# Time steps' sums and one group's y transposes one large product later; weights-stationary products in runs of sixteen matmuls of equal width

## The chip, the cores and the metric

The kernel runs on one core of one Trainium2 chip. The metric is the device time of one execution in microseconds (us); lower is better. Times are given as the median of several runs with the lowest and the highest. One further execution was taken by the hardware profiler; the profile's rows come from that one.

Five engines work in parallel, each through its own queue in order: TensorE (PE; its weight loads are shown apart as PEld), VectorE (DVE), ScalarE (ACT), GpSimd (POOL) and SyncE (SP, which here only starts DMAs). TensorE writes to PSUM, which has eight banks of 128 x 512 float32; VectorE and ScalarE read from there.

## The reference

It is a decoder trunk of two layers on 256 positions of width 1024. Each layer is a SwiGLU FFN (half step), a token mixer, a second FFN and a gated per-layer embedding. All weights and results are float32.

```python
for i in range(DEPTH):                                   # 2
    h = h + 0.5 * swiglu(rmsnorm(h, ffn1_norm[i]), ffn1_wg[i], ffn1_wu[i], ffn1_wd[i])
    h = h + hybrid_mixer(rmsnorm(h, mix_norm[i]), w_in[i], ...)
    h = h + 0.5 * swiglu(rmsnorm(h, ffn2_norm[i]), ffn2_wg[i], ffn2_wu[i], ffn2_wd[i])
    gate = jax.nn.sigmoid(rmsnorm(h, ple_norm[i]) @ ple_w_gate[i])
    h = h + gate * (p[i] @ ple_w_proj[i])
return rmsnorm(h, final_norm)

def hybrid_mixer(u, w_in, ...):
    proj = u @ w_in
    sc_b, sc_c, sc_x, m_z, m_xbc, m_dt, gate_a, gate_m = jnp.split(proj, PROJ_SPLITS, axis=-1)
    y_a = (sc_b * causal_depthwise_conv(sc_c * sc_x, sc_conv_w)) @ sc_w_out
    xbc = jax.nn.silu(causal_depthwise_conv(m_xbc, m_conv_w) + m_conv_b)
    xs, bm, cm = jnp.split(xbc, (SSM_INNER, SSM_INNER + SSM_GROUPS * SSM_STATE), axis=-1)
    dt = jax.nn.softplus((m_dt + m_dt_bias).astype(jnp.float32))
    y = ssd_chunked(xh * dt[..., None], A * dt, bm, cm)  # 32 heads, 4 groups, chunks of 128
    y = (y + m_D[:, None] * xh).reshape(b, s, SSM_INNER)
    y_m = grouped_rmsnorm(y * jax.nn.silu(m_z), m_norm, SSM_GROUPS) @ m_w_out
    merged = jax.nn.sigmoid(gate_a) * y_a + jax.nn.sigmoid(gate_m) * y_m
    return merged @ w_o
```

In `ssd_chunked` the running sums of `A * dt` within a chunk of 128 positions (`a_cum`) give the decays: within the chunk, to its end, and from one chunk to the next.

## The kernel before

**Products.** Each float32 operand is split into a high part (rounded to the fast float32 form, `hi`) and the rest (`lo`), and a product is made of three: hi x hi, hi x lo, lo x hi. The weights come in chunks of two halves, each 128 x 1024. SyncE fetches a half (`fetch`, L113), ScalarE makes `whi` and VectorE `wlo` of it (`half`, `split`, L94 to L127). Up to seven halves are live (`NHALF`), so the load runs over two chunks ahead of the product that reads them; a half's place is reused when its last reader on TensorE is done.

There are two forms. In the activations-stationary form (`as_`, L248) the activations are loaded into the array and 512 columns of weights stream past; all its matmuls have 512 columns. It makes the FFNs' down products, the head of each stage, z, the gates and the output products. In the weights-stationary form (`wide_ws`, L236) 128 columns of weights are loaded, and the activations of all 256 positions stream past. For `whi` the moving operand is `both[:, k]`, high and low part of the activations side by side, 512 columns; for `wlo` it is the high part alone, 256 columns. `xx` is the activations' tile. One such product takes one chunk: for each of two blocks of 128 output columns (b = 0, 1; one PSUM bank each) eight matmuls of 512 and eight of 256 columns over k = 0 to 7. The list `FOURS` (L234) orders each block's sixteen: 2 wide, 4 narrow, 4 wide, 4 narrow, 2 wide; block 0 is done before block 1 begins. Left and right half of a bank are then added up (ScalarE copies one half, VectorE adds the other: `both_parts`, L391, in the FFN; `Mixer.wide`, L843).

The FFN's up products use this form for chunks 4 to 21 (`up`, L406), and in the mixer it makes bc (4 products), xs (8) and sc (12).

`drip` (L208) puts small matmuls of the mixer's heads (`xd` times `m`, 64 columns, one per head) between those of the large products: `wide_ws` lets up to four go in the middle and up to four at the end of each block, `as_` two at its end.

**Order of the mixer.** `ORDER` (L40) is a list by hand of the forty large products of a mixer. After the n-th of them the small steps follow that `side` (L756) has for n. `EARLY = (1, 4)`: after product 1 `steps` (VectorE and ScalarE make `dt` and `av`), after product 4, sc0.1, `sums` (L936). `sums` has three fp32 products on TensorE with `av` (each shown as two matmuls), copies of them by VectorE (`acT`, `acum`, `w0`), two exponentials on ScalarE, and a DMA on ScalarE's queue that writes `acT` to DRAM as `acD`. `decay` later reads `acD` back, broadcast to all partitions, as `m`, by a DMA on ScalarE's queue too. Products 5 and 6 are bc10 and sc0.2.

For each group g of heads `LAGS[g]` (L43) says how many large products after the second xs product of g a step comes. For group 2 that product is xs5, number 21; `y_turn0` and `y_turn1` have lag 8, and so come after number 29, xs7. `y_turn` (L1036) transposes the finished y of one chunk on TensorE into one bank (`flip`, L271), ScalarE copies the bank to `yh`, and VectorE makes `yl` from bank and `yh`. Its input y comes from `gain` (L1032) on VectorE. Number 30 is z3.0 (activations-stationary; its two banks are held up to z3.1, number 33), and `turn0`, `overlap` and `decay0` of group 3 follow it; number 31 is gm0.0. ga1.0, number 28, holds two banks up to number 34.

The eight banks are one pool (`bank`, L76); a step that needs one waits until a former user's last reader is done. The framework that builds the program sets the order of instructions within each engine's queue by their dependences and their place in the program, so that on ScalarE and VectorE instructions of neighbouring steps are interleaved.

Of the kernel before, what the change touches and what calls it, by code (L numbers as in the profile page):

```python
# [16 lines left out]
P = 128  # L17
# [5 lines left out]
KD = D // P  # L23
# [15 lines left out]
LEAD = 8  # L39
ORDER = ("bc8 sc0.0 xs0 sc0.1 bc10 sc0.2 xs1 sc1.0 sc1.1 sc1.2 xs2 xs3 z1.0 sc2.0 sc2.1 z1.1 sc2.2 xs4 bc9 bc11 xs5 "  # L40
         "z2.0 z2.1 sc3.0 xs6 sc3.1 sc3.2 ga1.0 xs7 z3.0 gm0.0 so0.0 z3.1 ga1.1 gm0.1 so1.0 gm1.0 gm1.1 so0.1 so1.1").split()
EARLY = (1, 4)
LAGS = [  # L43
# [16 lines left out]
def trunk(ctx: ExitStack, tc: tile.TileContext, a: dict, out: bass.AP):  # L60
# [15 lines left out]
    def bank():  # L76
        return psp.tile([P, 512], F32, tag="ps", name=nm("ps"))

    def mm(o, l, r, start, stop):
        return nc.tensor.matmul(o, lhsT=l, rhs=r, start=start, stop=stop).ins  # L80
# [55 lines left out]
    def chunk(name, i, c, kn):  # L136

        key = (name, i, c)
        sources[key] = (a[name][i, c], kn)
        return key  # L140
# [67 lines left out]
    def drip(n=1):  # L208
        for _ in range(min(n, len(fill))):
            fill.pop(0)()  # L210
# [20 lines left out]

    FOURS = [(k, s) for s, ks in enumerate((range(2), range(4), range(2, 6), range(4, 8), range(6, 8))) for k in ks for s in (s % 2,)]  # L234

    def wide_ws(o, wc, cols, x):  # L236
        xh, _, both = x
        for n, (k, s) in enumerate(FOURS):
            if n == KD + 2:
                drip(KD // 2)  # L240
            if s == 0:
                mm(o, wc[k][0][:, cols], both[:, k], k == 0, k == KD - 1)
            else:
                mm(o[:, 0:256], wc[k][1][:, cols], xh[:, k], False, False)
        drip(KD // 2)


# [136 lines left out]
    class FFN:  # L384
        def __init__(self, i, gu, dn, gname, ple=None):
# [3 lines left out]
            hh, hl, banks, acc, head_pr = {}, {}, {}, {}, {}  # L389
# [7 lines left out]
            def evac(j):  # L397
                gate, pr = both_parts(banks[j][0], "sg"), both_parts(banks[j][1], "pr")
                del banks[j]
                nc.scalar.activation(gate, gate, AF.Silu)  # L400
                nc.vector.tensor_tensor(pr, gate, pr, op=ALU.mult)
                hh[j] = fp.tile([P, 256], F32R, tag=f"hh{j}", name=nm("hh"))
                hl[j] = fp.tile([P, 256], F32R, tag=f"hl{j}", name=nm("hl"))
                split(hh[j], hl[j], pr)

            def up(j):  # L406
                def f(wc):
                    banks[j] = [bank(), bank()]
                    for b in range(2):
                        wide_ws(banks[j][b], wc, slice(b * P, (b + 1) * P), prep.x)  # L410
                    evac(j)
                return f, [chunk(gu, i, j, KD)]

# [44 lines left out]
            n = NF // 2  # L458
# [141 lines left out]
    class Mixer:  # L600
        def __init__(self, i):
# [150 lines left out]
            for c in range(NT):  # L752
                small[f"turn{c}"] = lambda g, c=c: xs_turn(2 * g + c)
                for what in ("decay", "scale", "outputs", "skip", "chain", "gain", "y_turn"):
                    small[what + str(c)] = lambda g, c=c, f=getattr(S, what): f(g, c)
            side = {EARLY[0]: [S.steps], EARLY[1]: [S.sums]}  # L756
            for g in range(NG):
# [10 lines left out]
            def wide(name, x, done, kd=KD, upto=None, extra=()):  # L768
# [23 lines left out]
                if upto:  # L792
                    return acc, [([], [run(c, [0]) for c in range(nch - STAG, nch)]),
                                 ([run(c, [1]) for c in range(nch - STAG, nch - 1)], [run(nch - 1, [1])])]

            S.ym, S.mo_tail = wide("w_mo", of_y, None, kd=2 * KD, upto=True)
            S.wo = Narrow("w_o", i, lambda: S.mt)
            self.tail = S.wo.tail
# [44 lines left out]
        def wide(self, wc, what):  # L843

            pss = [bank(), bank()]
            for b in range(2):
                wide_ws(pss[b], wc, slice(b * P, (b + 1) * P), self.prep.x)
            v = self.t2(what)
            for b in range(2):
                o = v[:, b * 256:(b + 1) * 256]  # L850
                nc.scalar.activation(o, pss[b][:, 256:512], AF.Copy)
                nc.vector.tensor_tensor(o, o, pss[b][:, 0:256], op=ALU.add)
            return v
# [230 lines left out]
    for s in stages[1:] + [None]:  # L1084
        prep = s.prep if s else Last(a["final_norm"])
# [80 lines left out]
```

## Time and profile before

| | |
|---|---|
| median of 3 runs | 1535.74 us (1530.8 to 1536.1) |
| the profiled execution, time | 1531.25 us |
| the profiled execution, span | 1529.5 us |
| PE, DVE, ACT busy | 99%, 68%, 62% of the span |
| mean granted TensorE clock | 0.997 |
| DMA | 285.59 MB, 187 GB/s |

How to read it: the span goes from the first instruction to the last. A busy TensorE means that some matmul is under way; matmuls overlap, each being issued while the one before still drains, so their lengths (0.39 us for 512 columns) are longer than the distance of their starts, and the distance of the starts is the pace. In a row of the timeline stand the start, the length of the merged group, the engine, the line, the operation, the output and inputs by the program's names, the shapes and the count. Brackets show how long the engine sat idle before, and what ended that. The granted clock is 1.00 when TensorE runs at full speed.

### The profile page before, as it was taken

The numbers are of one execution on the slowest core, as the hardware profiler recorded it, in microseconds if no ns is written. First come the engines' busy times: TensorE is split into PE (matmuls) and PEld (weight loads), VectorE is DVE, ScalarE is ACT, GpSimd is POOL, SyncE is SP. The second block draws the span as 40 slices with busy tenths as digits, with TensorE's granted clock in tenths as the row PEclk, the third lists the DMA queues.
The fourth block names the chain that finished last, engine by engine and source line by source line (L and its number), as shares of the span: only waits on it lengthen the run. The fifth ranks groups of instructions, "written<-read, shape, count | busy, mean of one in ns | idle before, by whom it ended". The sixth has DMA issues, their size and how long they took to land.

```text
span 1529.5 us, 20958 instructions
## 1 busy us (share of the span) xinstructions
PE 1507.4 (99%) x7793; PEld 1272.1 (83%) x7793; DVE 1043.7 (68%) x1511; ACT 944.7 (62%) x1472; POOL 24.6 (2%) x41
## 2 busy tenths in 40 slices
PE   9999999999999999999999999999999999999998
PEld 6888887888888888888878888888888888888886
DVE  6666467989865576664676655688888555767545
ACT  6665367879854356653666654687888543666544
POOL 0000000000000000000000000000000000000000
PEclk9999999999999999999999999999999999999999
DMA  7656564556556556656565565655555565665642
GB/s 268 213 190 189 172 206 156 192 184 198 188 160 187 195 191 197 192 193 193 164 211 180 190 193 163 208 190 176 194 193 181 164 193 176 217 191 185 190 158 90
DMA packets 85432, 285.59 MB, mean 187 GB/s; under 512 B 10577, under 2 KB 10961, under 8 KB 85330
## 3 DMA queue, kind: packets, MB, share of 16 engines
q1 hardware_dynamic: 77968, 267.94, 54.5%
q10 hardware_dynamic: 7362, 16.31, 3.2%
q8 instruction: 61, 1.00, 0.3%
q14 instruction: 41, 0.34, 0.1%
HBM read 283.10 MB, written 1.11 MB: 186 GB/s over the span
## 4 chain that ended last, share of the span: by engine, by line
PE 90%; DVE 5%; ACT 2%; issue 2%; DMA 0%; POOL 0%; POOLq 0%; ACTq 0%; DVEq 0%
PE ps L80 88%; DVE wlo L96 3%; PE ps L277 1%; ACT whi L98 1%; DVE xn L333 1%; PE ps L638 0%; DMA m<-acD 0%; POOL rstd L293 0%; ACT junk L325 0%; DVE ac L863 0%; DVE xx L281 0%; ACT m L981 0%; PE ps L439 0%; DVE h L538 0%; DVE y L1034 0%
## 5 line engine op out<-in xcount | busy, mean ns | idle before, releaser
L96 DVE TENSOR_TENSOR wlo<-raw,whi 128x1024 fp32r<-128x1024 f32 x508 | 615.8, 1221 | 335.3 <-ACT whi L98 324.1
L98 ACT ACTIVATE whi<-raw 128x1024 fp32r<-128x1024 f32 x508 | 534.0, 1058 | 275.0 <-PE ps L80 241.5
L80 PE MATMUL ps<-xx,whi 128*128 128x512 f32 x1920 | 538.2, 398 | 0.0
L80 PE MATMUL ps<-whi,xx 128*128 128x512 f32 (+1 forms) x1168 | 369.7, 392 | 2.4 <-ACT whi L98 1.5
L80 PEld LDWEIGHTS ps<-xx,whi 128*128 128x128 f32 x1920 | 327.0, 189 | 45.5 <-issue 3.8
L80 PEld LDWEIGHTS ps<-xx,wlo 128*128 128x128 f32 x1920 | 294.5, 189 | 40.3
L80 PE MATMUL ps<-xx,wlo 128*128 128x256 f32 x1920 | 306.3, 281 | 0.0
L80 PEld LDWEIGHTS ps<-whi,xx 128*128 128x128 f32 x1168 | 217.9, 188 | 48.4 <-ACT whi L98 2.8
L80 PE MATMUL ps<-wlo,xx 128*128 128x512 f32 (+1 forms) x584 | 222.6, 388 | 0.3 <-DVE wlo L96 0.3
L80 PE MATMUL ps<-whi,hh 128*128 128x512 f32 x352 | 137.3, 390 | 0.0
L80 PE MATMUL ps<-wlo,hh 128*128 128x512 f32 x352 | 137.0, 389 | 0.0
L80 PEld LDWEIGHTS ps<-wlo,xx 128*128 128x128 f32 x584 | 109.9, 188 | 22.8 <-DVE wlo L96 1.8
L80 PE MATMUL ps<-whi,hl 128*128 128x512 f32 x352 | 113.7, 389 | 0.0
L80 PEld LDWEIGHTS ps<-whi,hl 128*128 128x128 f32 x352 | 66.1, 188 | 13.8
L80 PEld LDWEIGHTS ps<-wlo,hh 128*128 128x128 f32 x352 | 66.1, 188 | 13.7
L80 PEld LDWEIGHTS ps<-whi,hh 128*128 128x128 f32 x352 | 66.1, 188 | 13.6
L393 ACT ACTIVATE sg<-ps 128x256 f32<-128x256 f32 x72 | 27.7, 385 | 54.7 <-PE ps L80 54.7
L400 ACT ACTIVATE sg<-sg 128x256 f32<-128x256 f32 x72 | 30.0, 416 | 33.1 <-DVE sg L394 33.1
L80 PE MATMUL ps<-whi,yh 128*128 128x512 f32 x128 | 50.0, 390 | 0.0
L80 PE MATMUL ps<-wlo,yh 128*128 128x512 f32 x128 | 49.8, 389 | 0.0
L293 POOL TENSOR_TENSOR rstd<-var,mhalf 128x1 f32<-128x1 f32 x34 | 23.6, 696 | 1500.0 <-DVE var L287 998.5
L325 ACT ACTIVATE junk<-h 128x512 bf16<-128x512 f32 (+1 forms) x37 | 22.6, 612 | 39.3 <-DVE h L538 28.4
(162 smaller groups left out, 1209.1 us busy)
## 6 DMA issues: line engine op xcount, KB each, us to landing
raw<-in_gu SPq DMA_DIRECT2D x176, 512.0 KB, 4.2
raw<-in_dn SPq DMA_DIRECT2D x88, 512.0 KB, 3.9
raw<-in_w_xbc SPq DMA_DIRECT2D x48, 512.0 KB, 4.1
raw<-in_w_sc SPq DMA_DIRECT2D x48, 512.0 KB, 4.0
raw<-in_w_z SPq DMA_DIRECT2D x32, 512.0 KB, 3.7
raw<-in_w_mo SPq DMA_DIRECT2D x32, 512.0 KB, 3.7
raw<-in_w_ga SPq DMA_DIRECT2D x16, 512.0 KB, 4.3
m<-acD ACTq DMA_DIRECT2D x16, 512.0 KB, 4.6
```

The lines of the kernel that those rows point to most:

```text
L80: return nc.tensor.matmul(o, lhsT=l, rhs=r, start=start, stop=stop).ins
L96: return nc.vector.tensor_tensor(lo, src, hi.bitcast(F32), op=ALU.subtract).ins
L98: up = nc.scalar.activation(hi, src, AF.Copy).ins
L277: nc.tensor.transpose(tp[:, j * P:(j + 1) * P], src[:, c:c + P], ident)
L293: nc.gpsimd.tensor_tensor(r, v, mhalf, op=ALU.pow)
L325: self.squared = nc.scalar.activation(junk[:, 0:sl.stop - sl.start], h[t][:, sl], AF.Square, scale=1.0 / 32.0, accum_out=ss).ins
L333: ins = nc.vector.scalar_tensor_tensor(xn[:, sl], h[t][:, sl], r, g, op0=ALU.mult, op1=ALU.mult)
L393: nc.scalar.activation(v, ps[:, 256:512], AF.Copy)
L400: nc.scalar.activation(gate, gate, AF.Silu)
```

## The change

```diff
-EARLY = (1, 4)
+EARLY = (1, 5)
 LAGS = [
...
-     ("skip1", 4), ("y_turn0", 8), ("y_turn1", 8), ("chain1", 5), ("gain1", 6), ("gain0", 7),],
+     ("skip1", 4), ("y_turn0", 9), ("y_turn1", 9), ("chain1", 5), ("gain1", 6), ("gain0", 7),],
...
-    FOURS = [(k, s) for s, ks in enumerate((range(2), range(4), range(2, 6), range(4, 8), range(6, 8))) for k in ks for s in (s % 2,)]
-
-    def wide_ws(o, wc, cols, x):
+    LONG_RUNS = [(b, k, s) for s, ks in ((0, range(KD - 1)), (1, range(KD)), (0, range(KD - 1, KD))) for b in range(2) for k in ks]
+
+    def wide_ws(os, wc, x):
         xh, _, both = x
-        for n, (k, s) in enumerate(FOURS):
-            if n == KD + 2:
+        for n, (b, k, s) in enumerate(LONG_RUNS):
+            cols = slice(b * P, (b + 1) * P)
+            if n in (KD - 1, 2 * KD - 2, 3 * KD - 2):
                 drip(KD // 2)
             if s == 0:
-                mm(o, wc[k][0][:, cols], both[:, k], k == 0, k == KD - 1)
+                mm(os[b], wc[k][0][:, cols], both[:, k], k == 0, k == KD - 1)
             else:
-                mm(o[:, 0:256], wc[k][1][:, cols], xh[:, k], False, False)
+                mm(os[b][:, 0:256], wc[k][1][:, cols], xh[:, k], False, False)
         drip(KD // 2)
...
                     banks[j] = [bank(), bank()]
-                    for b in range(2):
-                        wide_ws(banks[j][b], wc, slice(b * P, (b + 1) * P), prep.x)
+                    wide_ws(banks[j], wc, prep.x)
                     evac(j)
...
             pss = [bank(), bank()]
-            for b in range(2):
-                wide_ws(pss[b], wc, slice(b * P, (b + 1) * P), self.prep.x)
+            wide_ws(pss, wc, self.prep.x)
```

The sums come after product 5, bc10, instead of 4, sc0.1. Group 2's two y transposes come after number 30, z3.0, instead of 29, xs7.

`wide_ws` now takes both banks and orders all 32 matmuls of a product: seven wide of block 0, seven wide of block 1, eight narrow of block 0, eight narrow of block 1, then the last wide one of each block. The next product begins with fourteen wide ones, so that where two such products follow each other without anything between, sixteen wide matmuls stand in a row, and sixteen narrow ones within each product. Both banks are complete only at the product's end. The head products may go in after matmul 7, 14, 22 and 32, four at a time, where before it was after 10 and 16 of each block.

## The prediction

> **What bounds the kernel now.** I read the page first, then the view of waits for TensorE, then its timeline. The page says that TensorE is nearly never without work:
>
> ```profile
> span 1529.5 us, 20958 instructions
> ...
> PE 1507.4 (99%) x7793; PEld 1272.1 (83%) x7793; DVE 1043.7 (68%) x1511; ACT 944.7 (62%) x1472; POOL 24.6 (2%) x41
> ...
> PE 90%; DVE 5%; ACT 2%; issue 2%; DMA 0%; POOL 0%; POOLq 0%; ACTq 0%; DVEq 0%
> ```
>
> So time can go in two ways only: TensorE's matmuls follow each other more closely, or its few waits vanish. The view of waits lists the latter (total us, times, longest):
>
> ```profile
> PE ps L80 <- DVE av L933: 5.5, 2, 2.8
> PE ps L277 <- DVE xn L333: 2.4, 5, 1.4
> PE ps L277 <- DVE y L1034: 2.0, 2, 1.0
> ...
> PE ps L80 <- ACT whi L98: 1.5, 3, 0.7
> ...
> PE ps L80 <- DVE wlo L96: 0.3, 1, 0.3
> ```
>
> The first row is the wait of the sums (they multiply `av`), once per layer; the third is that of group 2's y transposes, once per layer. The change moves exactly these two. The last row says that the split weights come in time almost always.
>
> For the pace I read TensorE's timeline in the first FFN (start, length, xcount), where the alternating runs of four stand alone:
>
> ```profile
> 121.09 1.09 PE L80 MATMUL ps<-xx,whi 128*128 128x512 f32 x4
> 122.02 0.64 PE L80 MATMUL ps<-xx,wlo 128*128 128x256 f32 x4
> 122.50 1.09 PE L80 MATMUL ps<-xx,whi 128*128 128x512 f32 x4
> ...
> 126.70 1.09 PE L80 MATMUL ps<-xx,whi 128*128 128x512 f32 x4
> ```
>
> I take starts, since lengths overlap. Four 512-column matmuls take 122.02 - 121.09 = 0.93 us, 0.2325 each; four of 256 columns 0.48, 0.120 each. From 121.09 to 126.70 lies one product (16 of each): 5.61 us. Where the up products end and the all-512 down products begin, the pace changes:
>
> ```profile
> 136.53 0.63 PE L80 MATMUL ps<-xx,whi 128*128 128x512 f32 x2
> 137.00 0.39 PE L80 MATMUL ps<-whi,hh 128*128 128x512 f32 x1
> ...
> 137.92 0.62 PE L80 MATMUL ps<-whi,hl 128*128 128x512 f32 x2
> ...
> 139.28 0.62 PE L80 MATMUL ps<-whi,hl 128*128 128x512 f32 x2
> ```
>
> 137.92 to 139.28 is one period of six: 1.36 us, 0.2267 each. The six from 136.53 to 137.92, right behind a run of 256, took 1.39. So a 512 run needs about six matmuls to settle, and loses about 0.03 us on the way. That this is no property of the weights-stationary form shows where such a product follows a long 512 run:
>
> ```profile
> 35.10 0.61 PE L80 MATMUL ps<-xx,whi 128*128 128x512 f32 x2
> 35.55 0.64 PE L80 MATMUL ps<-xx,wlo 128*128 128x256 f32 x4
> ```
>
> Its first two take 0.45 us, 0.225 each; only behind the first 256 run do they slow to 0.2325.
>
> **The runs of sixteen.** The change adds and drops no matmul. How many there are, by the page:
>
> ```profile
> L80 PE MATMUL ps<-xx,whi 128*128 128x512 f32 x1920 | 538.2, 398 | 0.0
> ...
> L80 PE MATMUL ps<-xx,wlo 128*128 128x256 f32 x1920 | 306.3, 281 | 0.0
> ```
>
> 1920 / 16 = 120 products: 18 in each of four FFNs, 24 in each of two mixers. Each goes from eight width changes to two. Afterwards 16 wide matmuls cost 16 x 0.2267 + 0.03 = 3.657 us. For a long run of 256 the trace has only the dt product, with half as many stationary columns:
>
> ```profile
> 221.53 2.03 PE L80 MATMUL ps<-xx,dtw 128*64 128x256 f32 x16
> 223.40 0.63 PE L80 MATMUL ps<-xx,whi 128*128 128x512 f32 x2
> ```
>
> 1.87 / 16 = 0.117 each. The narrow matmul with 128 columns is bounded by 0.117 and 0.120; I take 0.119, nearer the row with the same stationary shape: 1.904 us. The product becomes 5.561, a gain of 0.049. Some ten products are cut by interposed head products (the drips keep their count, four of four a product) and gain little, so I count 110: **-5.4 us**. Ends: with 0.117, 5.527 us and -9.5; if the wide run never settles (0.2325 x 16 + 1.904 = 5.624), +1.5.
>
> The Trainium skill, "TensorE: Matmul & The Clock Gate", section "Wait — 56ns, not 53.3ns?", speaks against this part: start to start is N / 2.4 GHz plus a fixed 2.5 ns or so, whatever stands beside it. By it (an estimate from that page) a product is 16 x 215.8 + 16 x 109.2 ns = 5.20 us in any order, and this term would be 0. The rows above disagree, in the size and in that the same width takes 0.225 or 0.2325 by its neighbours.
>
> What the new order does to others: both banks of a product now end with it, so the first bank's copy and add, which ran beside the second half, come 2.8 us later, in line with the second's. In an FFN they fit:
>
> ```profile
> 126.70:132.31 5.61, 5.61 (x34) 4.90 (x33) 3.96 (x7) 3.90 (x7) 0.00 (x0) 1.00 0.59 193
> ```
>
> VectorE is busy 3.96 and ScalarE 3.90 of the 5.61 us, and the output is needed only in the down stage, the bank four products on. I cost it at 0; cover gone, it is one copy more on the way, 385 ns:
>
> ```profile
> L393 ACT ACTIVATE sg<-ps 128x256 f32<-128x256 f32 x72 | 27.7, 385 | 54.7 <-PE ps L80 54.7
> ```
>
>  The low halves of the weights are first read at matmul 14 instead of 2, which only helps; the second high half is read at 4 instead of 8, about 0.5 us sooner, and the loads run over two products ahead.
>
> **The sums, one product on.** Windows of the two stalls (span, PE, PEld, DVE, ACT, POOL, granted clock, DMA):
>
> ```profile
> 246.00:250.00 4.00, 1.25 (x8) 0.60 (x6) 3.74 (x9) 3.58 (x6) 0.00 (x0) 1.00 0.33 110
> 250.00:257.60 7.60, 7.60 (x35) 6.59 (x36) 4.53 (x11) 2.81 (x6) 0.00 (x0) 0.78 0.70 225
> 1003.27:1007.30 4.03, 1.28 (x8) 0.68 (x6) 3.66 (x9) 3.50 (x6) 0.00 (x0) 1.00 0.37 117
> 1007.30:1014.00 6.70, 6.70 (x41) 5.92 (x41) 4.66 (x12) 3.40 (x8) 0.00 (x0) 1.00 0.73 213
> ```
>
> 4.00 - 1.25 and 4.03 - 1.28: 2.75 us idle each. Behind the first stall the granted clock is 0.78 over 7.6 us, 1.7 us lost; behind the second it is 1.00. One product on is 5.6 us, over twice the lateness, so both go: 5.5 + 1.7 = **-7.2 us**. The Trainium skill, same page, section "HAM oscillation — how this bites in real kernels", has the rule of no idle gaps over about 3.4 us. Read strictly it gives no loss to a gap of 2.75 and 1.7 us less to win (a sum of 1521); the first window disagrees, the third agrees.
>
> What is late next? The six fp32 matmuls of the sums, VectorE's copies, ScalarE's exponentials and one DMA write of `acD` move along. On ScalarE's queue the read of `m` waits for that write, and everything of ScalarE waits behind it:
>
> ```profile
> 254.65 1.28 ACT L950 ACT_TABLE_LOAD   x1 [2.45 <-DMA acD<-acT]
> ```
>
> Now the 2.45 us lie where ScalarE had little to do (2.81 of 7.60); afterwards they fall in the next product, before this one:
>
> ```profile
> 263.00:269.00 6.00, 6.00 (x35) 5.22 (x34) 5.71 (x9) 5.91 (x11) 0.00 (x0) 1.00 0.62 178
> ```
>
> ScalarE is full there. The weights are far enough ahead, but group 0's states product is not:
>
> ```profile
> 285.45 0.58 ACT L639 ACTIVATE xg<-ps 128x512 f32<-128x512 f32 x1
> ...
> 286.06 0.69 DVE L987 TENSOR_TENSOR xw<-xg,w 128x512 f32<-128x512 f32 x1 [0.17 <-ACT xg L639]
> ...
> 286.86 1.07 PE L80 MATMUL ps<-xw,btok 128*128 128x512 f32 x2
> ```
>
> `xw` ends at 286.75, and TensorE uses it at 286.86: no slack. A late ScalarE makes a new wait of 0 to 2.45 us a layer; I take 1.0, nearer the lower end, since ScalarE does the rest of its work with gaps: **+2.0 us**.
>
> **Group 2's y transposes.** In the first mixer:
>
> ```profile
> 414.06 0.74 DVE L1034 SCALAR_TENSOR_TENSOR y<-y,rstd,mn 128x512 f32<-128x512 f32 x1
> ...
> 414.95 1.06 PE L277 MATMUL ps<-ident,y 128*128 128x128 f32 x8 [1.01 <-DVE y L1034]
> ...
> 417.60 1.06 ACT L280 ACTIVATE yh<-ps 128x512 fp32r<-128x512 f32 x2
> ...
> 420.45 1.28 DVE L281 TENSOR_TENSOR yl<-ps,yh 128x512 fp32r<-128x512 f32 x2
> ...
> 422.25 0.48 PE L80 MATMUL ps<-whi,xx 128*128 128x512 f32 x1
> ```
>
> The wait of 1.01 goes, twice: -2.0. But the two banks are free only when `yl` is done, at 421.73, and the product gm0.0 starts at 422.25. Moved to after z3.0, the transposes stand 2.5 us or less before gm0.0, while ga1 and z3 hold two banks each and `turn0`, `overlap` and the two transposes the other four: all eight. gm0.0 must wait for one of these copies. Bounds 0 (copies at once: about 0.5 + 0.6 + 0.7 us) and 4 us (as late as here: 422.25 - 414.95 = 7.3, less 2.5, and some); I take 0.5 a layer, since VectorE has no `yl` of its own before it then: **-1.0 us** net.
>
> Sum: -5.4 - 7.2 + 2.0 - 1.0 = -11.6 on the profiled execution's 1531.25 us (span 1529.5): 1519.6, say **1520**. That execution is 4.5 us under the median of the three (1535.74; 1530.8 to 1536.1). A clock drop after the second layer's stall too would be 1.7 of it, and would go with the stall; the rest I can't place, so it is kept for the upper end.
>
> **Rivals.**
> 1. Both widths settle (narrow at 0.117): -9.5 instead of -5.4, 1515. For: the dt row; against: its loads are half as wide.
> 2. Spacing goes by a matmul's own width and form alone (0.2325 and 0.119 in these products, whatever the order): the runs give nothing, 1519.6 + 5.4 = 1525. For: products in both stages have one period; against: the rows at 35.10 and 137.92. (The rule of the Trainium skill on the gap, "TensorE: Matmul & The Clock Gate", is of this kind.)
> 3. The stalls move instead of going: states late by the full 2.45 us in both layers, gm0.0 by 2 us: 2 x 1.45 + 2 x 1.5 = 5.9 more, 1525.5. For: the full ScalarE, the full banks.
> 4. Slower: VectorE becomes the bound of the mixers. Its queue is in order; an add that waits for the product's end can hold up what stands behind it.
>
> ```profile
> 223.00:330.00 107.00, 103.99 (x591) 88.67 (x590) 89.09 (x163) 83.02 (x148) 1.72 (x2) 0.98 0.55 176
> ```
>
> It has 17.9 us to spare in 107, 19 products of 5.6 us: 0.94 us each. If the later first add costs it over 0.94 us in each of the 48 mixer products, the rest is paid; from 0.94 + 11.6 / 48 = 1.18 us on the kernel is slower, at 1.5 it is 1519.6 + 48 x 0.56 = 1546. Against: TensorE waited 0.3 us in all for `wlo`, and the weights run two products ahead.
>
> **How the numbers follow.** Chances: forecast 0.43, rival 1 0.17, rival 2 0.20, rival 3 0.13, rival 4 0.07. The range 1511 to 1529 takes in the first four with some microseconds around them (below: rival 1 with no new waits, 1512; above: rival 3 with most of the 4.5) and leaves out rival 4. Half a per cent, 7.7 us, is about what a measurement can tell: faster means under 1528. That is nearly all of the forecast and rival 1 (0.57 of 0.60), most of rival 2 (0.13) and half of rival 3 (0.07): 0.77. What is left of these is within: 0.03 + 0.07 + 0.06 = 0.16. Slower is rival 4, 0.07.
>
> **What would show it.** Right: product period 5.56 instead of 5.61; no row `av` and no `y` L1034 in the waits; clock 1.00 behind the sums. Wrong: a period of 5.61 or more (rival 2), 5.53 (rival 1), new rows of waits for `xw` L987, `yh` or `yl` (rival 3), or many waits for `wlo` in the mixers (rival 4).

## The result, and the profile after

The changed kernel takes 1522.28 us (median of 6 runs, 1521.07 to 1528.09); the kernel before, measured beside it, 1533.12 us (6 runs, 1530.8 to 1536.1). The ratio is 0.9935, with an interval of 0.9914 to 0.9957: about 10 us faster. The profiled execution took 1522.78 us, its span is 9.1 us shorter than before.

The page of the changed kernel, with the same rows as shown of before:

```profile
span 1520.4 us, 21065 instructions
...
PE 1501.2 (99%) x7793; PEld 1273.1 (84%) x7793; DVE 1045.9 (69%) x1511; ACT 915.6 (60%) x1468; POOL 21.6 (1%) x41
...
L80 PE MATMUL ps<-xx,whi 128*128 128x512 f32 x1920 | 472.1, 394 | 0.0
...
L80 PE MATMUL ps<-xx,wlo 128*128 128x256 f32 x1920 | 249.6, 283 | 0.0
```

The matmuls are the same 7793. That the two last groups' busy time fell from 844.5 to 721.7 us is no gain of 123 us: overlapping lengths are merged within a group, and longer runs overlap more with their like. The pace has to be read from starts. TensorE's timeline in the first FFN (start, length, count):

```profile
118.89 3.82 PE L80 MATMUL ps<-xx,whi 128*128 128x512 f32 x16
122.55 2.08 PE L80 MATMUL ps<-xx,wlo 128*128 128x256 f32 x16
124.46 2.91 PE L80 MATMUL ps<-xx,whi 128*128 128x512 f32 x12
```

(The last count is cut by the window.) Sixteen wide ones take 122.55 - 118.89 = 3.66 us, sixteen narrow ones 1.91, 0.12 each; a product 5.57 us instead of 5.61. With the trace's third decimal it is 5.566 against 5.613.

TensorE's waits (total us, times, longest):

```profile
PE ps L638 <- ACT xsil L864: 2.7, 2, 1.4
PE ps L278 <- DVE xn L334: 2.4, 5, 1.4
...
PE ps L80 <- ACT whi L98: 1.6, 3, 0.7
PE ps L80 <- DVE xw L986: 1.4, 3, 0.7
PE ps L80 <- DVE wlo L96: 0.8, 2, 0.5
```

The rows for `av` (5.5 us) and for group 2's `y` (2.0) are gone. New are `xsil`, read by group 1's transposes `turn0`, and `xw`, read by group 0's states. Both lie in the mixers, once or twice a layer.

The windows around the sums of the first layer (span, PE, PEld, DVE, ACT, POOL, granted clock, DMA) have neither idle time nor a lower clock:

```profile
244.00:250.40 6.40, 6.40 (x40) 5.75 (x40) 6.08 (x14) 4.47 (x6) 0.00 (x0) 1.00 0.53 149
250.68:258.28 7.60, 7.60 (x44) 6.51 (x43) 7.40 (x18) 6.30 (x13) 0.00 (x0) 1.00 0.69 256
```

**The balance of the span.** Taken from a product's first matmul to the matmul that follows its last, 81 of the 120 products gain 0.047 us, give or take 0.004. The others have matmuls of another kind beside or among theirs (transposes, states, head products; with sixteen head products inside, 7.80 us after and 7.78 before) and gain about 0.01 in the mean: 81 x 0.047 + 39 x 0.01 = 4.2. So -4.2 for the pace, -5.5 for `av`, -1.7 for the clock behind it, -2.0 for `y`, +2.7 for `xsil`, +1.4 for `xw`, +0.5 for `wlo`: -8.8, against 9.1 measured.

That list tells what was gained, not what brought it. The experiments ask for the latter: is it the new order inside a product, the moved sums, or the moved transposes?

One property of all profiles has to be known first. The first up product starts at about 35.0 us in some executions and at about 38.5 in others, of the same instructions before it. A span that starts late is 3.4 us too long for a comparison; this is told with each. (TensorE's rows show where the time goes: four matmuls of the opening, `ps<-row,ones`, begin between 5 and 6 us in both cases; they take 1.98 us in the kernel before and in the changed one, and 3.78 us in each of the four executions that start late.)

### The profile page after: what moved, and what is told of

Read it like the earlier page. It is cut to its first block, busy times and chain, and to the rows that moved or that the text cites. A ratio compares the mean times of both kernels' runs of the same rounds, so it can differ in the third digit from the quotient of the medians.

```text
span 1520.4 us, 21065 instructions
## 1 busy us (share of the span) xinstructions
PE 1501.2 (99%) x7793; PEld 1273.1 (84%) x7793; DVE 1045.9 (69%) x1511; ACT 915.6 (60%) x1468; POOL 21.6 (1%) x41
## 4 chain that ended last, share of the span: by engine, by line
PE 89%; DVE 5%; ACT 2%; issue 2%; DMA 1%; POOL 1%; SPq 0%; POOLq 0%; ACTq 0%; DVEq 0%
PE ps L80 87%; DVE wlo L96 2%; PE ps L278 1%; DMA raw<-in_gu 1%; POOL rstd L294 1%; DVE xn L334 1%; DVE ac L862 0%; DMA m<-acD 0%; ACT whi L98 0%; PE ps L638 0%; ACT m L980 0%; DVE xx L282 0%; ACT L864 0%; PE ps L439 0%; ACT junk L326 0%
## 5 line engine op out<-in xcount | busy, mean ns | idle before, releaser
L80 PE MATMUL ps<-xx,whi 128*128 128x512 f32 x1920 | 472.1, 394 | 0.0
L80 PEld LDWEIGHTS ps<-xx,whi 128*128 128x128 f32 x1920 | 350.8, 188 | 70.5 <-issue 4.3
L80 PEld LDWEIGHTS ps<-xx,wlo 128*128 128x128 f32 x1920 | 245.8, 191 | 8.9
L80 PE MATMUL ps<-xx,wlo 128*128 128x256 f32 x1920 | 249.6, 283 | 0.0
L96 DVE TENSOR_TENSOR hl<-pr,hh 128x256 fp32r<-128x256 f32 x72 | 30.6, 425 | 58.3 <-ACT hh L98 58.3
L980 ACT ACTIVATE m<-m,acum 128x128 f32<-128x128 f32 x128 | 41.2, 391 | 4.9 <-DMA m<-acD 4.9
```

What stands on the lines that cost most here:

```text
L96: return nc.vector.tensor_tensor(lo, src, hi.bitcast(F32), op=ALU.subtract).ins
L980: nc.scalar.activation(m[:, hh], m[:, hh], AF.Relu, scale=-1.0, bias=self.acum[:, r0 + hh:r0 + hh + 1])
```

## Experiments

All ratios are against the kernel before, run on the same chip; its medians were 1534.23 us (29 runs) for the first four experiments, 1533.81 (29) for the next four and 1535.59 (15) for the last four.

| | median, us | ratio, interval | span, first up product | waits of the mixers' steps, us |
|---|---|---|---|---|
| new order alone | 1526.24 | 0.9942, 0.9927 to 0.9958 | 1520.2, 34.6 | `av` 3.2, `xw` 1.5 |
| sums alone | 1534.05 | 0.9997, 0.9986 to 1.0007 | 1533.4, 38.5 | `xw` 6.2, `y` 2.0 |
| y transposes alone | 1532.55 | 0.9983, 0.9970 to 0.9997 | 1530.6, 35.6 | `av` 5.5 |
| both banks late, runs of four | 1532.14 | 0.9985, 0.9975 to 0.9996 | 1530.0, 35.2 | `xw` 6.3, `wlo` 1.1 |
| one wide, one narrow | 1538.63 | 1.0024, 1.0010 to 1.0038 | 1535.2, 35.0 | `xw` 5.3, `xsil` 2.7 |
| runs of eight | 1534.78 | 1.0007, 0.9994 to 1.0020 | 1534.4, 38.5 | `xsil` 10.2 |
| `turn0` later | 1518.55 | 0.9897, 0.9881 to 0.9913 | 1514.4, 35.0 | none |
| `turn0` and states later | 1537.96 | 1.0026, 1.0014 to 1.0039 | 1534.1, 35.2 | `st` 10.4 |
| sums alone, `acT` by ScalarE | 1525.22 | 0.9935, 0.9921 to 0.9949 | 1523.4, 35.2 | `xw` 1.8, `y` 2.0 |
| best, y as before | 1520.65 | 0.9902, 0.9887 to 0.9917 | 1518.6, 38.5 | `xw` 0.3 |
| best, sums as before | 1528.37 | 0.9952, 0.9940 to 0.9965 | 1524.5, 34.8 | `av` 3.2, `m` 1.7, `xw` 1.5 |
| narrow run first | 1532.17 | 0.9979, 0.9968 to 0.9989 | 1532.1, 38.5 | `av` 6.7, `y` 0.9 |

### The three parts one by one

The new order alone is the changed kernel with the sums and the transposes put back:

```diff
-EARLY = (1, 5)
+EARLY = (1, 4)
-     ("skip1", 4), ("y_turn0", 9), ("y_turn1", 9),
+     ("skip1", 4), ("y_turn0", 8), ("y_turn1", 8),
```

> Only the new order of matmuls; sums and y transposes where they were before. Theory (a change of width costs about 17 to 20 ns per pair of changes, and one pair per product is left of four): product period 5.566 us instead of 5.613, 120 x 0.047 = 5.6 us less, the waits for av (5.5 us) and y (2.0 us) stay, span near 1524. Rival (spacing by own width alone): period 5.61, span 1529.5. For the new wait of 2.7 us for xsil: if the new order makes it, it stands here too (span near 1526.5); if the earlier sums' end makes it, it is absent.

The sums alone, in the kernel before:

```diff
-EARLY = (1, 4)
+EARLY = (1, 5)
```

> Only the sums one product later. Theory: no wait for av, granted clock 1.00 behind the sums, 5.5 + 1.7 = 7.2 us less, span near 1522.3, product period 5.613. Rival (the stall moves): new waits for xsil or xw of 2 to 4 us in the first half of the mixers, span near 1526.

And the y transposes alone, in the kernel before:

```diff
-     ("skip1", 4), ("y_turn0", 8), ("y_turn1", 8),
+     ("skip1", 4), ("y_turn0", 9), ("y_turn1", 9),
```

> Only group 2's y transposes one product later. Theory: the wait of 2.0 us for y goes and nothing comes in its place, span near 1527.5. Rival (eight banks full at gm0.0): a wait for yl, yh or xg at gm0.0 of 0.5 to 2 us a layer, span 1528.5 to 1531.

**The order alone gives as much as the whole change**: 0.9942 beside 0.9935, intervals overlapping. Its period is 5.566 us too, but it does more than the pace can: the wait for `av` shrank although the sums stand where they stood. TensorE's waits in this kernel:

```profile
PE ps L80 <- DVE av L932: 3.2, 2, 1.6
...
PE ps L80 <- DVE xw L986: 1.5, 2, 0.8
```

1.6 us a layer instead of 2.75, no row for `y`, and the clock at 1.00 behind the sums in both layers. So -4.2 for the pace, -2.3 for `av`, -1.7 for the clock, -2.0 for `y`, +1.5 for `xw`: -8.7. Its profile began 0.5 us earlier than that of before and is 9.3 us shorter, so 8.8 are to be explained.

Why does `av` come earlier? It ends a long chain on VectorE that begins with an exponential on ScalarE, `sp_e`. ScalarE's timeline of the kernel before, and then of the new order alone:

```profile
233.93 1.06 ACT L98 ACTIVATE whi<-raw 128x1024 fp32r<-128x1024 f32 x1 [1.07 <-PE ps L80]
...
238.25 0.26 ACT L913 ACTIVATE sp_e<-sp_e 128x64 f32<-128x64 f32 x1
```

```profile
236.12 0.26 ACT L912 ACTIVATE sp_e<-sp_e 128x64 f32<-128x64 f32 x1
```

Before, ScalarE stood for 1.07 us at the head of its queue until TensorE gave a half's place free (the split `whi` writes there), and `sp_e` waited behind it. With the new order none of ScalarE's splits in the nine microseconds ahead of `sp_e` waits for TensorE. At the other end of the chain VectorE's timeline of before has two splits of weights, `wlo`, ahead of `av`, that of the new order one:

```profile
246.39 1.22 DVE L96 TENSOR_TENSOR wlo<-raw,whi 128x1024 fp32r<-128x1024 f32 x1
...
247.66 1.22 DVE L96 TENSOR_TENSOR wlo<-raw,whi 128x1024 fp32r<-128x1024 f32 x1
248.79 0.29 DVE L933 SCALAR_TENSOR_TENSOR av<-dt,negA 128x32 f32<-128x32 f32 x2
```

```profile
245.00 1.21 DVE L96 TENSOR_TENSOR wlo<-raw,whi 128x1024 fp32r<-128x1024 f32 x1
246.14 0.28 DVE L932 SCALAR_TENSOR_TENSOR av<-dt,negA 128x32 f32<-128x32 f32 x2
```

From the first dt matmul (221.53 before, 220.15 in the new order) to `av` that is 27.3 and 26.0 us; up to `sp_e` it is 16.72 and 15.97, so 0.75 of the 1.3 us lie ahead of `sp_e` and the rest behind it. Nothing but the order of matmuls was changed in this kernel, and it changed how weight splits and the mixer's small work interleave on two other engines. The rows point to the places: by the two lists the first high half of a product has its last reader at matmul 24 of 32 before, and at matmul 11 in the new order. But the new order also completes the first bank only at the product's end, and ScalarE's copy of that bank, `xsb`, which stood ahead of `sp_e` before (at 232.48), now stands behind it (at 236.29). This kernel doesn't tell the two apart.

**The sums alone are worth nothing**: 0.9997. The wait for `av` went, and one for `xw` came that is longer:

```profile
PE ps L80 <- DVE xw L987: 6.2, 2, 3.1
```

The rows of VectorE show where it comes from. TensorE issues the sums at 255.47; what VectorE does next, with the last of its rows the copy that reads their bank, and the DMA on ScalarE's queue that follows:

```profile
258.74 1.22 DVE L96 TENSOR_TENSOR wlo<-raw,whi 128x1024 fp32r<-128x1024 f32 x1
259.88 2.45 DVE L863 SCALAR_TENSOR_TENSOR ac<-bcv,convw,ac 128x255 f32<-128x255 f32 x6
262.24 0.28 DVE L943 COPY acT<-ps 64x128 f32<-64x128 f32 x1
```

```profile
262.55 0.51 ACTq L945 DMA_DIRECT2D acD<-acT  x1
```

From the sums to the copy pass 6.8 us, where it was about 1 us before and in the changed kernel: a product later the sums land behind the convolution of bc10 in VectorE's queue. With `acD` late, the read of `m` and everything of ScalarE behind it are late, and group 0's states wait. Rival 3's mechanism, at more than its price. Behind the second layer's wait the clock fell too (0.83 over the ten us from 1045.00): -5.5 for `av`, -1.7 for the clock behind it, +6.2 and +1.7 for the new ones make +0.7, and without its late start the span is 0.5 us over that of before.

**The y transposes alone** are worth what their wait was: the row is gone, no new one appears, and the ratio 0.9983 is -2.6 us (-4.6 to -0.5). The one profiled execution, 1530.6 us, doesn't show it: it began 0.5 us later, and the clock, which fell behind `av` in one layer before, fell in both (0.51 from 251.20 to 254.60, 0.50 from 1005.60 to 1012.40).

### Was it VectorE's queue? `acT` copied by ScalarE

This is the kernel with the sums alone, and one line more:

```diff
-            nc.vector.tensor_copy(acT, aps[0:W2, 128:256])
+            nc.scalar.activation(acT, aps[0:W2, 128:256], AF.Copy)
```

> As the run with the sums alone moved, but ScalarE instead of VectorE copies acT out of PSUM. Theory (alone moved, the sums won nothing because their copy stood behind 4.6 us of other work in VectorE's queue, so that acD, m and xw came late): acD is written within 2 us of the sums, the wait of 6.2 us for xw shrinks to 2 us or less, span near 1528 to 1529. Rival (xw is late because VectorE and ScalarE have too much to do before it): the wait stays at 5 to 6 us, span near 1533.

ScalarE's rows, and the waits:

```profile
254.28 0.26 ACT L943 ACTIVATE acT<-ps 64x128 f32<-64x128 f32 x1
254.57 0.51 ACTq L945 DMA_DIRECT2D acD<-acT  x1
```

```profile
PE ps L80 <- DVE xw L987: 1.8, 2, 0.9
```

`acD` is written at 254.57 instead of 262.55; this execution began 3.3 us earlier, so 4.7 of the 8.0 are the edit's. The wait falls from 6.2 to 1.8 us, the clock stays at 1.00 behind it, and the ratio falls from 0.9997 to 0.9935. One copy on another engine makes of a worthless move one that is worth as much as the whole change, with the old pace.

### How the pace depends on the runs

Three kernels keep the changed one's sums, transposes and late banks, and change only the list. Runs of four, as before, but both banks ending with the product (s is 0 for a wide matmul, 1 for a narrow one):

```python
LONG_RUNS = [(b, k, s) for s, bks in (
    (0, [(0, 0), (0, 1)]), (1, [(0, k) for k in range(4)]), (0, [(0, k) for k in range(2, 6)]), (1, [(0, k) for k in range(4, 8)]),
    (0, [(0, 6), (1, 0), (1, 1), (1, 2)]), (1, [(1, k) for k in range(4)]), (0, [(1, k) for k in range(3, 7)]), (1, [(1, k) for k in range(4, 8)]),
    (0, [(0, 7), (1, 7)])) for b, k in bks]
```

> Sums and y transposes as in the changed kernel; matmuls in runs of four again (eight changes of width per product), but so ordered that both banks end with the product, as in the changed kernel. Theory: product period back at 5.61, span 5.6 us over that of the changed kernel, near 1526. Rival (the gain of the new order is not the width changes but that low halves are read late or both banks end together): period 5.566, span near 1520.4. For the xsil wait: it stays if late banks make it, and goes if the early reading of the high halves (a weights copy placed ahead in ScalarE's queue) makes it.

One wide and one narrow by turns:

```python
WIDES = [(b, k, 0) for b in range(2) for k in range(7)] + [(0, 7, 0), (1, 7, 0)]
NARROWS = [(b, k, 1) for b in range(2) for k in range(8)]
LONG_RUNS = [m for pair in zip(WIDES[:15], NARROWS[:15]) for m in pair] + [NARROWS[15], WIDES[15]]
```

> The changed kernel with the same 32 matmuls of a product in the order one wide, one narrow, so that 30 of 32 neighbours differ in width. Theory (each pair of changes costs a fixed 17 to 20 ns): 5.546 + 15 x 0.017 = 5.80 us a product, 28 us more than the changed kernel in all, near 1548. A weaker form (the loss is a settling of the pace that has no time to develop within one matmul): about 16 x (0.2345 + 0.1185) = 5.65 us, 10 us more. Rival (own width alone): 5.57 as in the changed kernel, no difference in all.

And runs of eight:

```python
LONG_RUNS = [(b, k, s) for s, bks in (
    (0, [(0, k) for k in range(6)]), (1, [(0, k) for k in range(8)]), (0, [(0, 6)] + [(1, k) for k in range(7)]),
    (1, [(1, k) for k in range(8)]), (0, [(0, 7), (1, 7)])) for b, k in bks]
```

> The changed kernel with runs of eight: four changes of width a product instead of two. Theory: 5.546 + 2 x 0.020 = 5.586 us a product, 0.020 more than with runs of sixteen, 2.4 us in all. Rival (the runs of four lose by their first matmuls only in part, the pace settles over ten matmuls): 5.60.

TensorE's timeline with one by one, then with runs of eight (the same place of two products that follow each other; the counts are cut by the windows):

```profile
120.37 0.63 PE L80 MATMUL ps<-xx,whi 128*128 128x512 f32 x2
...
126.02 0.63 PE L80 MATMUL ps<-xx,whi 128*128 128x512 f32 x2
```

```profile
119.94 2.00 PE L80 MATMUL ps<-xx,whi 128*128 128x512 f32 x8
...
125.53 0.86 PE L80 MATMUL ps<-xx,whi 128*128 128x512 f32 x3
```

5.65 and 5.59 us. With third decimals, and 16 x 0.2266 + 16 x 0.120 = 5.546 us for settled matmuls:

| changes of width in a product | 2 | 4 | 8 | 30 |
|---|---|---|---|---|
| period, us | 5.566 | 5.586 | 5.613 | 5.653 |
| above 5.546, ns | 20 | 40 | 67 | 107 |

A pair of changes costs about 20 ns as long as the runs are long enough to settle (2 and 4 changes), and less each in shorter runs, where the settling is cut off. A fixed price of 20 ns per pair would put 30 changes 300 ns above settled, at about 5.85; spacing by a matmul's own width alone would leave all four equal. Both fall.

Two by-results. With both banks late and runs of four the kernel isn't slower than before (0.9985). It has both moves in it, which alone gave 0.9997 and 0.9983 with early banks: that VectorE's adds come late costs the mixers nothing that can be measured, and rival 4 falls. And the runs of eight, 0.027 us a product better than before, lose it all in one wait, which is 1.4 us a layer in the changed kernel and 5.2 here, and in the clock, which stood at 0.50 around it (303.50 to 310.30, and 1061.30 to 1068.10):

```profile
PE ps L640 <- ACT xsil L866: 10.2, 2, 5.2
```

### Is it the pace, or what comes free when?

The last doubt on the new order: perhaps the faster pace itself brings `av` closer. A kernel with the same two changes per product and the old places of sums and transposes, in which the narrow run comes early, tells these apart:

```diff
-    LONG_RUNS = [(b, k, s) for s, ks in ((0, range(KD - 1)), (1, range(KD)), (0, range(KD - 1, KD))) for b in range(2) for k in ks]
+    LONG_RUNS = [(b, k, s) for s, ks in ((0, range(1)), (1, range(KD)), (0, range(1, KD))) for b in range(2) for k in ks]
...
-            if n in (KD - 1, 2 * KD - 2, 3 * KD - 2):
+            if n in (KD + 2, 2 * KD + 2, 3 * KD + 1):
```

> As the run of the new order alone, still runs of sixteen, but two wide matmuls, the sixteen narrow ones, then fourteen wide ones: the high halves are read late and stay occupied, the low ones are read early. Theory of the pace: 5.566 us a product as before. Theory of the sums (they are reached with a shorter wait under the new order because the high halves come free early, so ScalarE needn't wait for TensorE ahead of the exponential of the time steps): the wait for av is back at 5 us or more. Rival (any order with runs of sixteen has it): 3.2 us.

Its period is 5.566, as in the new order alone, its ratio 0.9979 and not 0.9942. The waits and ScalarE's timeline:

```profile
PE ps L80 <- DVE av L932: 6.7, 2, 3.3
```

```profile
236.45 0.39 ACT L850 ACTIVATE xsb<-ps 128x256 f32<-128x256 f32 x1 [1.85 <-PE ps L80]
237.18 1.06 ACT L98 ACTIVATE whi<-raw 128x1024 fp32r<-128x1024 f32 x1 [0.34 <-PE ps L80]
...
241.50 0.26 ACT L912 ACTIVATE sp_e<-sp_e 128x64 f32<-128x64 f32 x1
```

The same pace, twice the wait for `av`, and the clock low behind both. Where most of the high halves are read last, a split that waits stands ahead of `sp_e` again, and `sp_e` comes at 241.50 instead of 236.12; 3.9 us of that are the later start of this execution, 1.5 the order. So of the new order's 8.8 us the pace is about half (4.2); the rest comes with where in the order the matmuls stand. That it is the places of the halves alone is not shown. The first high half's last reader is now matmul 28 of 32, but the first bank too is complete seven matmuls before the product's end, and its copy, the row of `xsb`, stands ahead of `sp_e` again.

### The new waits, and the best of the kernels

ScalarE's timeline of the changed kernel at the wait for `xsil`, with that of before behind it:

```profile
295.98 1.06 ACT L98 ACTIVATE whi<-raw 128x1024 fp32r<-128x1024 f32 x1 [1.92 <-PE ps L80]
297.05 1.28 ACT L864 ACT_TABLE_LOAD   x1
298.35 0.63 ACT L864 ACTIVATE xsil<-ac 128x512 f32<-128x512 f32 x1
```

```profile
299.38 1.28 ACT L865 ACT_TABLE_LOAD   x1 [2.82 <-DVE ac L863]
300.68 0.63 ACT L865 ACTIVATE xsil<-ac 128x512 f32<-128x512 f32 x1
```

Before, ScalarE waited for `ac` alone. Now a split of weights that waits 1.92 us for TensorE stands ahead of it, and then the table load; VectorE has `ac` ready at 296.15, so the split makes 0.9 us of the wait of 1.4. Neither the new order alone nor the sums alone has a wait for `xsil`, and the runs of four with late banks have none: it takes the new order and the moved sums together. Since it is `turn0` of group 1 that waits, with lag 0, the remedy is to let it wait a product longer:

```diff
-    [("turn0", 0), ("overlap", 0), ("decay0", 1),
+    [("turn0", 1), ("overlap", 0), ("decay0", 1),
```

> The changed kernel with group 1's first turn (the transposes that wait for xsil) one product later. Theory (xsil is late because a weights copy that waits for TensorE stands ahead of it in ScalarE's queue; a product of 5.6 us covers 1.4): the wait of 2.7 us goes, span near 1517.7. Rival (the wait moves on, to xw of group 1 or to a later step): span stays near 1520.4, with a new row of 1 to 3 us.

This is the best kernel of all, 1518.55 us, 0.9897. Of TensorE's waits none for the mixers' small steps remains; the largest in total is now this, at the norms between the stages:

```profile
PE ps L278 <- DVE xn L334: 2.5, 5, 1.4
```

Its span is 6.0 us below the changed kernel's; `xsil` and `xw` are 4.1 of them. A wait also costs TensorE a little beyond its length: in the kernel before, the product that ends in the wait for `y` takes 6.78 us, 5.61 and 1.01 and 0.16 more. For the five waits that went this makes about 0.8 us; the remaining 1.1 I can't place.

A step of the same kind, taken on top of it, does harm. Here the states of group 0 come a product later too:

```diff
-     ("states", 3), ("carry", 4), ("skip1", 4),
+     ("states", 4), ("carry", 5), ("skip1", 5),
```

(`LAGS[0]`, cut to what differs.)

> As the run before it, and group 0's states, carry and second skip one product later too. Theory: the waits for xsil (2.7 us) and for xw (0.9 us of the 1.4) go, span near 1516.8. Rival (the waits move on to carry's result or group 0's chain): span 1518 to 1521.

```profile
PE ps L80 <- ACT st L992: 10.4, 2, 5.4
```

The next step, which reads `st`, now waits 5.4 us a layer; on ScalarE, `st` stands behind these, in one queue:

```profile
294.75 1.06 ACT L98 ACTIVATE whi<-raw 128x1024 fp32r<-128x1024 f32 x1 [2.91 <-PE ps L80]
297.25 0.40 ACT L980 ACTIVATE m<-m,acum 128x128 f32<-128x128 f32 x1 [1.45 <-DMA m<-acD]
...
299.49 0.58 ACT L992 ACTIVATE st<-ps 128x512 f32<-128x512 f32 x1
```

Two more start from the best kernel and take one move of the change back. First the y transposes (lags 8 again):

> The run with group 1's first turn later (1514.4 span), with the y transposes back at their old place. Theory (with runs of sixteen y is in time even at the old place, as in the run of the new order alone): no wait for y, span within 1 us of 1514.4. Rival (the move is worth what it was alone): a wait of 2.0 us for y, span near 1516.5.

Then the sums (`EARLY = (1, 4)` again):

> The run with group 1's first turn later (1514.4 span), with the sums back after product 4. Theory (the move of the sums pays only if the steps behind it are in time): waits of 3.2 us for av and up to 1.5 for xw as in the run of the new order alone, span near 1518 to 1519. Rival (what pays is the later turn alone): span near 1514.4.

Without the y move the ratio is 0.9902, as with it: under the new order its wait is gone anyway. Without the sums' move it is 0.9952 instead of 0.9897: there the move is worth its full price, since the copy of `acT` comes about a microsecond behind the sums. (The span is 1524.5 us where at most 1519 was expected; the wait for `m` and a fall of the clock in the first layer were not foreseen.) So the same edit is worth nothing in the kernel before and half a per cent in this one.

## Why the prediction was right, and which steps were not

The forecast was 1520 us, the result 1522.28; faster by over 0.5% was the likeliest. By its steps (span, us):

| step | forecast | measured |
|---|---|---|
| runs of sixteen, the pace | -5.4 | -4.2 |
| wait for `av`, and the clock behind it | -5.5 - 1.7 | -5.5 - 1.7 |
| new waits of the heads | +2.0 | +4.1 |
| group 2's y | -2.0 | -2.0 |
| gm0.0 waiting for a bank | +1.0 | 0 |
| `wlo` | 0 | +0.5 |
| sum | -11.6 | -8.8 (span: -9.1) |

**The runs of sixteen: right.** 5.566 us where 5.561 was forecast. The narrow matmul settles at 0.120, not 0.117 (rival 1 falls), and the width of neighbours does count (rival 2 falls). The Trainium skill, "TensorE: Matmul & The Clock Gate", section "Wait — 56ns, not 53.3ns?", has the distance of starts as N / 2.4 GHz plus about 2.5 ns whatever the neighbours are; the four periods above disagree. Only the number of products with the full gain was too high: 81 instead of 110, and the other 39 gained 0.01 each.

**"What the new order does to others … I cost it at 0": the step that failed.** I considered there what late banks could cost TensorE, and they do cost it nothing that can be measured. I did not ask how the other engines' queues change when halves and banks come free at other times. The order alone shortened the wait for `av` by 2.3 us and took that for `y` away, the clock stayed up, and it cost 1.5 at `xw`: about as much again as the pace. Most of what I put down to the two moves came with the order too; the total is right because the same waits can vanish only once.

**The sums: the two waits did go, but not for the reason given.** "One product on is 5.6 us, over twice the lateness" holds for `av`. For what comes behind it I named ScalarE's wait for `acD` as the danger and took the lateness from the row of before, 2.45 us. How late `acD` is, is set ahead of it by VectorE's queue: 6.8 us behind the sums in the old order, about 1 us in the new. That the changed kernel escaped this, the profile of before could not show. So the -7.2 us of this term came out by luck: in the old order the same move is worth nothing (0.9997).

**The new wait of +2.0: mis-sized.** It measures 4.1: 1.4 at `xw`, as foreseen (forecast 2.0), and 2.7 at `xsil`, which I had not on the list. The lateness there is not that of `acD` but a split of weights that waits for TensorE, ahead of a table load.

**gm0.0: wrong, and harmless.** I had it wait for one of eight banks. TensorE's timeline of the changed kernel behind z3.0:

```profile
414.69 1.03 PE L278 MATMUL ps<-ident,y 128*128 128x128 f32 x8
...
416.47 0.47 PE L80 MATMUL ps<-whi,xx 128*128 128x512 f32 x1
```

TensorE goes on at once, and not with gm0.0 but with the first half of z3.1, product 33, whose banks are held already. (ScalarE takes the silu of that half at 419.52; before, no half of group 3 was ready earlier than 436.7.) The framework ordered TensorE's own queue anew, so the scarcity of banks that I had counted was met by other work.

**Rivals 3 and 4.** Rival 3 (the stalls move) is what the sums alone do, at 6.2 us. Rival 4 (VectorE bound by late adds) did not occur, and the runs of four with late banks show it without the help of the pace.

**Left open.** Why the pace takes some six matmuls to settle, no run shows. Of the effects on `av`, 0.75 us ahead of `sp_e` and 0.5 behind it, no run separates what the places of the halves do from what the later first bank does. And why the runs of eight make `xsil` so late is read only from the queue, where the work on `m`, which waited 2.00 us for the DMA that reads `acD`, stands ahead of it.

## What to carry to other kernels

An order of matmuls is also an order in which buffers and banks come free: before costing a reordering at its pace alone, ask for each operand when its last reader now stands, and what is queued behind the instruction that waits for its place. A step moved "where there is time" is worth only what its slowest follower allows; try it with that follower on another engine before discarding it, and alone before praising it. In a change of several parts run each part by itself: here one part gave as much as all of them, one gave nothing, and the best kernel came from moving a step that was not part of the change.

## What the runs showed of the hardware

A wide matmul is not spaced by its own width alone: 0.2266 us settled, 0.2325 in runs of four beside narrow ones, about 20 ns lost with each pair of changes of width as long as the runs are long enough to settle.

The clock follows short waits, but not always. Windows behind the sums (granted clock in the third column from the end) in the new order alone, where the first layer's wait was 1.6 us; in the best kernel with the sums as before, 1.6 us too; in the narrow run first, both layers, 3.3 us; and in the kernel with late states, behind 5.4 us:

```profile
247.00:257.00 10.00, 10.00 (x56) 8.60 (x57) 8.66 (x19) 8.17 (x16) 0.00 (x0) 1.00 0.61 204
```

```profile
247.00:252.00 5.00, 5.00 (x17) 4.02 (x17) 3.22 (x8) 1.63 (x5) 0.00 (x0) 0.66 0.85 289
```

```profile
252.50:262.00 9.50, 9.50 (x49) 8.33 (x50) 6.06 (x14) 5.30 (x11) 0.00 (x0) 0.82 0.48 165
1008.00:1018.00 10.00, 10.00 (x43) 8.70 (x44) 5.38 (x14) 4.54 (x10) 0.00 (x0) 0.69 0.46 150
```

```profile
299.30:309.50 10.20, 9.38 (x31) 7.67 (x32) 7.24 (x14) 9.36 (x20) 0.00 (x0) 0.50 0.18 70
```

The same 1.6 us cost 5.00 x 0.34 = 1.7 us in one kernel and nothing in the other; behind 5.4 us the clock stayed low so long that 9.38 x 0.50 = 4.7 us of TensorE's busy time went. The Trainium skill, "TensorE: Matmul & The Clock Gate", section "HAM oscillation — how this bites in real kernels", allows idle gaps of up to some 3.4 us; the second window disagrees. Windows laid around a fall alone show it at half speed, for about 3.4 us or two or three times that: the last one above, and in the kernel before

```profile
251.20:254.60 3.40, 3.40 (x13) 2.83 (x12) 3.10 (x8) 0.91 (x2) 0.00 (x0) 0.50 0.67 206
```

So one fall costs 1.7 us or a multiple of it. A wait taken away is therefore worth its length and, now and then, 2 to 5 us more.

The start of an execution varies: the first up product comes at about 35.0 or 38.5 us. That is as much as the pace gains in 70 products; it may be a good part of what single runs of one kernel differ by, but only the profiled ones show their start.
